# Attention without a shifted copy of V: another order of scores, turns of 64x64, and another order of work in the last pair

## The chip, the cores and the metric

The kernel runs on one core of one Trainium2 chip. Its time is device microseconds of one launch. The text uses these engine names: PE is TensorE (matmul; PEld is its weight load), DVE is VectorE, ACT is ScalarE, POOL is GpSimd, SP is SyncE, which here only issues DMAs.

## The reference, cut to what matters

One decoder layer in float32: 2048 positions, width 1024, 16 attention heads of 64 and 16 SSD heads of 64. Attention is causal, with windows of 128 steps at dilations 1, 4 and 16; the three results are mixed by their softmax sums.

```python
def dilated_window_attention(q, k, v, slopes, dilation):
    # positions are split into `dilation` residue sequences, blocks of 128;
    # a block of queries sees its own block of keys and the one before
    scores = jnp.einsum('bnqrhe,bnkrhe->bnrhqk', qb, kk).astype(jnp.float32)
    ...
    valid = (jk >= 0) & (steps >= 0) & (steps <= ATT_STEPS)
    scores = jnp.where(valid[:, None, None], scores + bias, -jnp.inf)
    lse = jax.nn.logsumexp(scores, axis=-1)
    p = jnp.exp(scores - lse[..., None]).astype(vv.dtype)
    o = jnp.einsum('bnrhqk,bnkrhe->bnqrhe', p, vv)

def reference(x, w_in, ...):
    proj = jnp.einsum('bsd,de->bse', x, w_in[layer])
    q, k, v, z_att, z_ssm, xbc, dt_raw = jnp.split(proj, list(SPLITS), axis=-1)
    ...   # three dilations, o1 to o3 and l1 to l3
    wts = jax.nn.softmax(jnp.stack([l1, l2, l3], axis=0), axis=0)
    y_att = wts[0][..., None] * o1 + wts[1][..., None] * o2 + wts[2][..., None] * o3
    y_att = rms_norm(y_att.reshape(Bsz, S, D_ATT) * jax.nn.silu(z_att), att_norm_g[layer])
    ...   # conv, silu, ssd_chunked
    y_ssm = rms_norm(y.reshape(Bsz, S, D_SSM) * jax.nn.silu(z_ssm), ssm_norm_g[layer])
    out = jnp.einsum('bse,ed->bsd', jnp.concatenate([y_att, y_ssm], axis=-1), w_out[layer])
    x = layer_norm(alpha * x + out, ln_g[layer], ln_b[layer])
```

## The kernel before

The program has three stages. The first, up to about 1148 us, makes all projections, the convolution and the SSD branch, and leaves q, k, v, the gates, the SSD rows (`d_us`) and the prepared output weights (`d_wo`) in DRAM. The change does not touch it.

The second is the attention. It goes over eight pairs of heads, and in each pair over the three dilations `d` = 0, 1, 2 (strides 16, 4, 1), four quarters `qd` and two halves `half`: 192 steps of two blocks of 128 queries for two heads. The order of all engines is the order of the code. The loop handles the scores of step i, the turns of step i-2 and the values of step i-3. A step works thus:

- `scores` (L947): q times k into two PSUM banks `S`, one per head. Head h lies in the rows 64h to 64h+63 of the array and the half a of a query block in the columns 64a to 64a+63, so these matmuls are 64x64 and there are four places in the array for them. A block in the first position of its sequence has 128 keys; any other has 192 here, since each half of 64 queries sees three blocks of 64 keys. The half a=0 sees the keys -2, -1, 0 and a=1 sees -1, 0, 1 (in blocks of 64).
- DVE adds the table of slopes and takes the row minimum (L953), ACT takes the exponential and its sum (L962).
- `transposes`: four turns of 128x128 through the identity into a bank `T` (L976), copied by DVE to `PT` (L978). The third block of 64 keys of both query blocks (columns 128 to 255 of `P`) needs two more turns per step, one per head (L984), copied to `PC` (L987). Only steps with a block that is not first have them.
- `values` (L1002): `PT` and `PC` times v into two banks `N`, then ACT or DVE copies them to `num`. For `PC` to meet the right rows of v, v is there twice: `v` as it is and `vs`, shifted by 64 positions.

The loads of `v` and `vs` are 1 MB each, issued by POOL or SP. Between steps the loop also places, for the pair before, the mixing weights: `statistics` and `gather` (sums to DRAM and back in another layout), `weights` (DVE, ACT, POOL), `broadcast` (the weights read back over 64 partitions each), `combine` (POOL; in the last pair DVE) and `keep_u` (the finished rows to `d_ua`). `broadcast` begins with a one-element memset on DVE (L1087), which takes the buffer `wb`; that buffer may still be on its way to `d_ua`.

The third stage is the output product. 64 products (`product`, L1201 to L1203, 24 matmuls of 512 columns each) take 16 blocks of 128 positions times an SSD half and an attention half of the width times two halves of the output. The first eight are the SSD halves of blocks 0 to 3; they need `split` (a rounded part by ACT, L1167, and the rest by DVE or POOL, L1169) and the weights 8 to 15. The ninth is the attention half of block 0; it needs all of the last pair's `combine`. `load_w` brings the weights into buffers of the attention as those come free, on POOL's queue.

## Time and profile before

| What | Value |
|---|---|
| time, median of 3 runs | 2009.96 us (2007.39 to 2012.77) |
| profiled execution, its own time | 2003.82 us |
| its span | 2002.0 us |
| PE busy in the span | 1945.7 us, 97% |
| DVE, ACT, POOL busy | 64%, 56%, 50% |
| DMA | 447.67 MB, mean 224 GB/s |

The profile is one execution. A busy PE means that a matmul is under way, and in fp32 two matmul records stand for one matmul instruction (one for a turn in transpose mode). The timeline merges neighbouring instructions of one line, so a row's start tells more than its length: the time from one row's start to the next is what the work took on PE.

### The profile page before, as it was taken

Reading aid. Unit: us, or ns where it says so; the run is one execution under the profiler, and the core shown is the slowest. Engines: PE = TensorE matmul, PEld = TensorE weight load, DVE = VectorE, ACT = ScalarE, POOL = GpSimd, SP = SyncE. Lnnn points to the kernel's source line nnn. Section 1 sums busy time; section 2 is a strip of 40 time slices with the busy share of each in tenths; the row PEclk is TensorE's granted clock in tenths of the full one; section 3 lists DMA queues with packets and bytes.
Section 4 is the critical chain, followed back from the end, with each engine's and each line's share of the span. In section 5 each row is a group of like instructions: output and inputs, shape, how many; then the busy total and the mean of one; then the engine's idle time right before and its main releaser. Section 6 shows DMA issues by size and latency. Waiting matters only on the chain.

```text
span 2002.0 us, 42714 instructions
## 1 busy us (share of the span) xinstructions
PE 1945.7 (97%) x16008; PEld 1588.2 (79%) x16008; DVE 1275.8 (64%) x3204; ACT 1120.0 (56%) x3036; POOL 998.3 (50%) x877
## 2 busy tenths in 40 slices
PE   8999999999999999999999999999999888999998
PEld 7888899888888888988888877777777666888886
DVE  7655376887766655644454388888887736655553
ACT  5454343566556774456566488988888732322220
POOL 0366514666556667155565343676776622432221
PEclk9999999999999999999999999999999998999999
DMA  6788676566787876888888766888888988332210
GB/s 270 236 284 293 213 280 227 159 195 190 237 306 266 279 245 239 312 269 256 272 277 259 256 228 165 229 244 235 252 238 254 265 242 260 134 102 92 92 61 32
DMA packets 260656, 447.67 MB, mean 224 GB/s; under 512 B 44785, under 2 KB 146673, under 8 KB 249057
## 3 DMA queue, kind: packets, MB, share of 16 engines
q1 hardware_dynamic: 170912, 205.39, 32.2%
q0 software_dynamic: 39088, 142.54, 21.6%
q10 hardware_dynamic: 50448, 97.01, 15.7%
q8 instruction: 126, 2.06, 0.4%
q14 instruction: 82, 0.66, 0.1%
HBM read 301.85 MB, written 151.39 MB: 226 GB/s over the span
## 4 chain that ended last, share of the span: by engine, by line
PE 85%; DVE 5%; DMA 4%; ACT 3%; issue 2%; POOL 1%; SPq 0%; ACTq 0%; DVEq 0%; POOLq 0%
PE pp L260 13%; PE pp L264 13%; PE pp L262 13%; PE N L1002 7%; PE S L947 6%; PE T L976 5%; PE pp L309 4%; PE S L1201 4%; PE S L1203 4%; PE S L1202 3%; PE ss L309 2%; PE T L1201 2%; PE T L1203 2%; PE T L1202 2%; PE ss L627 2%
## 5 line engine op out<-in xcount | busy, mean ns | idle before, releaser
L217 POOL TENSOR_TENSOR w<-wr,w 128x512 fp32r<-128x512 f32 x217 | 285.6, 1327 | 268.2 <-ACT w L216 184.0
L962 ACT ACTIVATE P<-P,st 128x192 f32<-128x192 f32 (+1 forms) x768 | 323.4, 423 | 59.9 <-DVE st L953 55.4
L252 ACT COPY ev<-pp 128x512 f32<-128x512 f32 x200 | 117.1, 587 | 315.3 <-PE pp L264 281.5
L953 DVE CUSTOM_DVE_ANT_0 P<-S,tb 128x192 f32<-128x192 f32 (+1 forms) x768 | 205.8, 324 | 53.6 <-PE S L947 44.1
L272 DVE TENSOR_TENSOR ev<-pp,ev 128x512 f32<-128x512 f32 x152 | 101.2, 686 | 140.6 <-PE pp L264 95.9
L216 ACT CAST w<-wr 128x512 fp32r<-128x512 f32 x224 | 134.1, 620 | 23.5 <-DVE wr L211 11.9
L962 ACT ACTIVATION_READ_ACCUMULATOR P<-P,st 128x1 f32 x768 | 145.0, 189 | 0.0
L1111 POOL TENSOR_TENSOR wb<-num,wb 128x2048 f32<-128x2048 f32 x21 | 95.7, 4558 | 93.7 <-DMA wb<-d_wd 90.2
L978 DVE COPY PT<-T 128x512 f32<-128x512 f32 x192 | 131.7, 686 | 3.8 <-PE T L976 3.8
L976 PE MATMUL T<-ident,P 128*128 128x128 f32 x768 | 127.3, 288 | 6.7 <-DVE PT L978 4.5
L1002 PE MATMUL N<-PT,v 128*64 128x64 f32 (+1 forms) x1536 | 124.5, 259 | 4.2 <-DVE PT L978 3.5
L976 PEld LDWEIGHTS T<-ident,P 128*128 128x128 f32 x768 | 81.3, 141 | 52.9 <-ACT P L962 16.8
L211 DVE TENSOR_TENSOR wr<-wr 128x512 f32<-128x512 f32 x128 | 112.2, 877 | 9.3 <-DMA wr<-w 5.9
L947 PE MATMUL S<-k,ex 64*64 64x192 f32 (+1 forms) x2048 | 108.8, 322 | 3.2 <-issue 3.2
L1002 PEld LDWEIGHTS N<-PT,v 128*64 128x64 f32 x1536 | 79.4, 138 | 38.3 <-issue 22.7
L459 DVE SCALAR_TENSOR_TENSOR ss<-U,cw,ss 128x512 f32<-128x512 f32 x144 | 106.0, 752 | 2.9 <-ACT ss L455 0.6
L1177 DVE TENSOR_REDUCE tb<-P 128x128 f32<-128x1024 f32 x30 | 60.2, 2006 | 45.1 <-ACT P L1174 21.1
L1239 POOL TENSOR_TENSOR k<-k,wb 128x1024 f32<-128x1024 f32 x8 | 25.8, 3225 | 122.0 <-DVE k L1238 122.0
L587 ACT ACTIVATE mt<-csb,wdr 128x128 f32<-128x128 f32 x256 | 78.9, 395 | 0.9 <-PE ss L627 0.8
L947 PEld LDWEIGHTS S<-k,ex 64*64 64x64 f32 x2048 | 66.4, 134 | 15.4 <-issue 8.9
L596 DVE TENSOR_TENSOR mt<-mt,ss 128x1024 f32<-128x1024 f32 x32 | 39.0, 1220 | 54.1 <-ACT mt L592 53.7
L260 PE MATMUL pp<-TT4h,w 128*128 128x512 f32 x176 | 69.6, 395 | 0.0
(493 smaller groups left out, 5991.1 us busy)
## 6 DMA issues: line engine op xcount, KB each, us to landing
wr<-w ACTq DMA_DIRECT2D x164, 256.0 KB
d_wc<-w SPq DMA_DIRECT2D x48, 512.0 KB
w<-d_wc POOLq DMA_DIRECT2D x48, 512.0 KB, 6.4
wb<-d_wd SPq DMA_DIRECT2D x48, 512.0 KB
d_wo<-wot POOLq DMA_DIRECT2D x32, 512.0 KB, 4.3
csb<-d_cs ACTq DMA_DIRECT2D x32, 512.0 KB
d_wv<-w SPq DMA_DIRECT2D x14, 1024.0 KB
w<-d_wv POOLq DMA_DIRECT2D x14, 1024.0 KB, 8.7
```

What stands on the lines that cost most here:

```text
L216: nc.scalar.copy(h, r)
L217: low.tensor_tensor(l, r, h.bitcast(F32), op=OP.subtract)
L260: nc.tensor.matmul(ps, w[:, 0, k], th[:, k], start=start and k == 0, stop=False, skip_group_check=not start)
L262: nc.tensor.matmul(ps, w[:, 0, k], tl[:, k], start=False, stop=False, skip_group_check=not start)
L264: nc.tensor.matmul(ps, w[:, 1, k], th[:, k], start=False, stop=(k == 3), skip_group_check=not start)
L309: nc.tensor.matmul(o, (th, tl)[j == 1][:, k, t], w[:, int(j == 2), k], start=start and r % 2 == k == j == 0, stop=(k == 3 and j == 2), ski ...
L947: nc.tensor.matmul(o, A["q"][d][64 * h:64 * h + 64, blk, 64 * a:64 * a + 64], kv, start=True, stop=True)
L953: nc.vector.tensor_tensor_reduce(P[:, h, cs], sp[h][:, cs], t, -0.125, 3.0e38, OP.add, OP.min, accum_out=stat(A, 0, d, h, blk))
L962: nc.scalar.activation(p, p, AF.Exp, bias=stat(A, 0, d, h, blk), scale=-1.0, accum_out=stat(A, 1, d, h, blk))
L976: nc.tensor.transpose(tp[:, h, i], P[:, h, 256 * i:256 * i + 128], ident)
L978: nc.vector.tensor_copy(pt, tp)
L1002: nc.tensor.matmul(o, l, r, start=start, stop=True, skip_group_check=True)
```

## The change

`vs` goes, with its loads and its shifted tables. Each half of a query block now lays its three blocks of keys in another order: a=0 as -2, -1, 0 as before, a=1 as 0, 1, -1. So the scores of a=1 are two matmuls, of 128 and of 64 columns, where there was one of 192; those of 64 columns come after the four wide ones of the block. The third block of keys now lies for half a in the rows 64a, and is turned with matmuls of 64x64 against the identity (two heads, two blocks, two halves: eight of them) instead of two turns of 128x128. `N` is now one bank per half a, and the copies to `num` follow that.

Around it: `keep_u` moves from the step (1,0,0) to (0,0,1). In the last pair the weights 8, 9 and 10 go to the three `vs` buffers during pairs 5 and 6, others move; the SSD rows of blocks 0 to 3 are fetched in the attention loop and block 0 is split there from the end of dilation 4; `zt7` is loaded there too; the weights' broadcasts go ahead of `keep_u` and of residuals 2 and 3; the residuals go through SP instead of ACT; and block 3 is split after the first `combine` step instead of after the third.

```diff
-        def load_v(A, x, d, queue=nc.gpsimd):
+        def load_v(A, d, queue=nc.gpsimd):
...
         def keys(A, d, qd, bq, h, a):
...
-            lo, hi = (j, j + 2 * w) if f else (j + w * (a - 2), j + w * (a + 1))
-            k = k[:, 4 * bq:4 * bq + 4, lo:hi] if d == 1 else k[:, :, lo:hi]
-            return k.rearrange("p r (c j) -> p c r j", j=4)
+            parts = [(0, j, j + 2 * w)] if f else [(0, j, j + 2 * w), (128, j - w, j)] if a else [(0, j - 2 * w, j + w)]
...
         def scores(A, d, qd, half):
...
-                for h in range(2):
-                    for a in range(2):
-                        o, kv = sp[h][64 * a:64 * a + 64, cs], keys(A, d, qd, 2 * i + half, h, a)
...
+                for n in range(2):
+                    for h in range(2):
+                        for a in range(2):
+                            for c0, c1, kv in keys(A, d, qd, 2 * i + half, h, a)[n:n + 1]:
...
         def transposes(d, qd, half, P):
...
-            tc_ = psT.tile([128, 2, 2, 128], F32, name="T")
+            tc_ = psT.tile([128, 2, 2, 64], F32, name="T")
             for h in range(2):
-                nc.tensor.transpose(tc_[:, 0, h], P[:, h, 128:256], ident)
-            pc = io.tile([128, 2, 128], F32, name="PC", bufs=2)
-            rows = slice(64 * new[0], 128)
-            nc.vector.tensor_copy(pc[rows], tc_[rows, 0])
+                for i in range(new.start, new.stop):
+                    for a in range(2):
+                        r = slice(64 * a, 64 * a + 64)
+                        nc.tensor.matmul(tc_[r, h, i], P[r, h, 192 * i + 128:192 * i + 192], ident[r, r],
+                                         start=True, stop=True)
+            pc = io.tile([128, 2, 2, 64], F32, name="PC", bufs=2)
+            nc.vector.tensor_copy(pc[:, :, new], tc_[:, :, new])
...
-                    if pr > 1 and at == (1, 0, 0):
+                    if pr > 1 and at == (0, 0, 1):
                         keep_u(pairs[pr - 2], nc.sync)
...
+                    if pr == 7:
+                        if at == (1, 1, 0):
+                            free.append(big("q_0"))
+                            X = big("ex", F32)
+                            for j in range(2):
+                                fetch_raw(j, 1, X[:, j * D:j * D + D])
+                        if at in ((1, 2, 1), (1, 3, 0)):
+                            split(0, 1, slice(4 - 4 * half, 8 - 4 * half), (0,))
+                        if at == (2, 0, 0):
+                            split(0, 1, parts=(1,))
...
+                        if at in ((2, 2, 1), (2, 3, 0)):
+                            fetch_raw(qd, 1)
...
                 if i == 2:
-                    for j in range(2):
-                        scaled(j)
-                    add(*adds.pop(0))
-                    add(*adds.pop(0))
-                    for j in range(3):
-                        combine(A, j)
+                    combine(A, 0)
                     load_w(0, 0, "num")
...
                         os_.insert(0, big("k_1", F32))
+                        broadcast(A, 0)
                         for n in range(2):
                             residual(n)
+                        broadcast(A, 1)
+                        broadcast(A, 2)
+                        keep_u(pairs[6], nc.sync)
+                        for n in range(2, 4):
+                            residual(n)
+                    if i == 3:
+                        for n in range(2):
+                            scaled(n)
+                        add(*adds.pop(0))
+                        add(*adds.pop(0))
+                        combine(A, 1)
+                        load_w(1, 0, "num")
+                        combine(A, 2)
```

How this stands on the engines is shown at three places.

On PE, one step of dilation 1 late in the last pair, before: from the scores of one step to the values of another (`S`, `T` and `N` are PSUM banks, `PT` and `PC` the turned scores).

```order
L947 MATMUL S<-k,ex 64x192 x8
L976 MATMUL T<-ident,P 128x128 x4
L984 MATMUL T<-ident,P 128x128 x2
L1002 MATMUL N_19558<-PT,v 64x64 x2
L1002 MATMUL N_19558<-PT,vs 64x64 x2
L1002 MATMUL N_19559<-PT,vs 64x64 x2
L1002 MATMUL N_19559<-PT,v 64x64 x2
L1002 MATMUL N_19558<-PC,v 64x64 x2
L1002 MATMUL N_19559<-PC,vs 64x64 x2
L1002 MATMUL N_19558<-PC,vs 64x64 x2
L1002 MATMUL N_19559<-PC,v 64x64 x2
```

And now. The five rows of scores shown are those of the step's second block; the same five stand ahead of them for its first block.

```order
L947 MATMUL S<-k,ex 64x192
L947 MATMUL S<-k,ex 64x128
L947 MATMUL S<-k,ex 64x192
L947 MATMUL S<-k,ex 64x128
L947 MATMUL S<-k,ex 64x64 x2
L976 MATMUL T<-ident,P 128x128 x4
L987 MATMUL T<-ident,P 64x64 x8
L1009 MATMUL N_20774<-PT,v 64x64 x2
L1009 MATMUL N_20775<-PT,v 64x64 x2
L1009 MATMUL N_20774<-PT,v 64x64 x2
L1009 MATMUL N_20775<-PT,v 64x64 x2
L1009 MATMUL N_20774<-PC,v 64x64 x2
```

The scores grew from 8 matmuls to 12, the extra turns from two of 128x128 to eight of 64x64; the values are 16 matmuls as before.

On DVE, after the attention: the rows from the last of the mixing weights (`cm`) over the `combine` products (`wb<-num,wb`) to the split of block 3 (`num<-P,num`), before.

```order
L1080 TENSOR_TENSOR cm<-cm,mm 128x3x32
L1177 TENSOR_REDUCE tb_19839<-P 128x128
L1212 RECIPROCAL st<-st 128x1 x2
L1218 SCALAR_TENSOR_TENSOR k<-S,st,k 128x512 x2
L1111 TENSOR_TENSOR wb<-num,wb 128x2048 x2
L1115 TENSOR_TENSOR wb<-wb 128x2048
L1169 TENSOR_TENSOR num<-P,num 128x1024
```

And now, where the split of block 3 is `q<-P,q`.

```order
L1085 TENSOR_TENSOR cm<-cm,mm 128x3x32
L1181 TENSOR_REDUCE tb_20975<-P 128x128
L1216 RECIPROCAL st<-st 128x1 x2
L1115 TENSOR_TENSOR wb<-num,wb 128x2048
L1173 TENSOR_TENSOR q<-P,q 128x1024
L1222 SCALAR_TENSOR_TENSOR k<-S,st,k 128x512 x2
L1115 TENSOR_TENSOR wb<-num,wb 128x2048
L1119 TENSOR_TENSOR wb<-wb 128x2048
```

The split stands behind one `combine` product instead of two and a sum.

On SP, the DMAs at the end of the attention, before: the SSD rows (`d_us`), the statistics, the weights out and their broadcasts in.

```order
L1155 DMA P<-d_us_108 128x512
L1155 DMA P<-d_us_109 128x512
L1055 DMA d_st_119<-sT 16x16x8 x4
L1081 DMA d_wd_127<-cm 128x3x32
L1089 DMA wb<-d_wd_127 64x2048 x6
```

And now, with `d_ua` the rows of pair 6 and `xc` the residuals, which both were on ACT's queue.

```order
L1060 DMA d_st_119<-sT 16x16x8 x4
L1086 DMA d_wd_127<-cm 128x3x32
L1095 DMA wb<-d_wd_127 64x2048 x2
L1185 DMA k<-xc 128x1024 x2
L1095 DMA wb<-d_wd_127 64x2048 x2
L1095 DMA v<-d_wd_127 64x2048 x2
L1102 DMA d_ua<-wb 128x16x128
L1185 DMA ex<-xc 128x1024 x2
```

The first broadcast stands right behind the weights, and the store of `d_ua` and two residuals behind all broadcasts.

More of the change, by code (lines that the diff above doesn't have):

```diff
@@ L920, in cols @@
         def cols(d, qd, half, i):
-            w = 128 if first(d, qd, 2 * i + half) else 192
-            return slice(384 - w, 384) if i else slice(0, w)
+            return slice(192 * i, 192 * i + (128 if first(d, qd, 2 * i + half) else 192))
         def keys(A, d, qd, bq, h, a):
@@ L1004, in values @@
                 m = at(2 * i + half)
+                if d == 0:
+                    for h in range(2):
+                        mm(out(i, h), v[:, m, 64 * h:64 * h + 64], pt[:, h, i], half == 0)
+                    continue
+                f = first(d, qd, 2 * i + half)
+                for a in range(2):
+                    for h in range(2):
+                        mm(out(i, h, a), v[:, m if f else m - 1 + a, 64 * h:64 * h + 64],
+                           pt[:, h, i, 64 * a:64 * a + 64], half == i == 0)
+            for i in range(2):
                 if first(d, qd, 2 * i + half):
-                    for h in range(2):
-                        mm(out(i, h, 0, 128), v[:, m, 64 * h:64 * h + 64], pt[:, h, i], half == 0)
                     continue
@@ L1010, in values @@
                     for h in range(2):
[L1011 to L1021 removed]
+                        r = slice(64 * a, 64 * a + 64)
+                        mm(out(i, h, a), v[r, at(2 * i + half) - a, 64 * h:64 * h + 64], pc[r, h, i], False)
             if half == 1:
@@ L1296, in hybrid_layer @@
                         if pr == 7:
-                            for e in range(12, 16):
+                            for e in (14, 15):
                                 load_w(e, 1)
@@ L1316, in hybrid_layer @@
                         load_z(pairs[pr - 1])
-                    if pr == 7 and at in ((2, 0, 1), (2, 1, 0)):
-                        split(0, 1, slice(4 * qd, 4 * qd + 4), (0,))
-                    if pr == 7 and at == (2, 1, 0):
-                        split(0, 1, parts=(1,))
+                    if pr == 7:
[8 more added lines that the diff above has]
+                            split(0, 1, parts=(1,))
+                            zt7 = cm_.tile([128, NR, NJ], F32, name="num", bufs=6)
+                            nc.sync.dma_start(f2(zt7), d_za[7])
+                        if at in ((2, 2, 1), (2, 3, 0)):
+                            fetch_raw(qd, 1)
+                    if not half:
+                        for e, hf, name in LOADS.get((pr, d, qd, 0), ()):
+                            load_w(e, hf, name)
+                    if pr == 7 and at == (2, 0, 0):
+                        free.append(big("num"))
                     if at in STEPS:
@@ L1331, in hybrid_layer @@
                         permute(pairs[pr + 1], 1)
[L1332 to L1343 removed]
+        with tc.manual_schedule(engines={E.PE, E.DVE, E.Activation, E.Pool, E.SP}):
             A = pairs[7]
```

116 lines of the change are left out of this document (44 added, 72 removed).

## The prediction

> **What bounds the kernel now.** I read the windows first, cut where the stages of the trace change: attention, the passage to the output products, the products. The columns are the stretch, its length, busy time and instruction count of PE, PEld, DVE, ACT and POOL, PE's granted clock, the DMA share and GB/s.
>
> ```profile
> 1148.00:1596.00 448.00, 431.72 (x8082) 320.06 (x8082) 372.52 (x1898) 385.19 (x1717) 284.95 (x239) 1.00 0.81 233
> 1596.00:1673.00 77.00, 59.08 (x346) 46.21 (x344) 36.55 (x47) 20.46 (x34) 27.35 (x26) 0.84 0.93 261
> 1673.00:2002.00 329.00, 319.28 (x1403) 258.76 (x1401) 179.45 (x243) 78.73 (x112) 89.68 (x37) 0.99 0.30 99
> ```
>
> In the attention PE is busy 431.7 of 448 us, ACT 385 and DVE 373. So PE bounds it, with 16.3 us idle at most to be won, and work added on PE lengthens it while DVE and ACT have room. The passage is different: PE is idle 18 us of 77 and its clock is at 0.84. In the products PE is full again and the change adds nothing there.
>
> Next, PE's timeline for one full step of a smaller dilation, from its scores to the next step's scores (columns: start, length, engine, line, operation, count; rows left out are more of the same values).
>
> ```profile
> 1361.69 0.83 PE L947 MATMUL S<-k,ex 64*64 64x192 f32 x16
> 1362.46 0.66 PE L976 MATMUL T<-ident,P 128*128 128x128 f32 x4
> 1362.95 0.38 PE L984 MATMUL T<-ident,P 128*128 128x128 f32 x2
> 1363.27 0.34 PE L1002 MATMUL N<-PT,v 128*64 128x64 f32 x4
> ...
> 1363.88 0.27 PE L1002 MATMUL N<-PC,v 64*64 64x64 f32 x2
> ...
> 1364.16 0.85 PE L947 MATMUL S<-k,ex 64*64 64x192 f32 x16
> ```
>
> No row has a wait, so the differences of starts are prices: scores 0.77, four turns 0.49, two turns 0.32, PT values 0.61, PC values 0.28, in all 2.47 us. A step of the first dilation has no extra turns, and there the four turns are followed at once by the values:
>
> ```profile
> 1334.47 0.65 PE L976 MATMUL T<-ident,P 128*128 128x128 f32 x4
> 1335.06 0.66 PE L1002 MATMUL N<-PT,v 128*64 128x128 f32 x8
> ```
>
> That is 0.59 for the same four turns, 0.10 more. The difference is that the next matmul has another shape of stationary block (128*64 after 128*128). So **a change of shape costs 0.10**. It lies in 0.32 and 0.61 too, but not in 0.28, since PC values and scores are both 64*64. Then eight matmuls of 64 columns cost 0.51 where two run at once (PT, two column halves) and 0.28 where four do (PC, four quarters): 0.23 for four groups more, 0.058 a group.
>
> **The turns.** Two turns of 128x128 become eight of 64x64, row half a to column half a, so two places of the array are used and two can run at once. The nearest row is PT: eight matmuls of 64 columns, two at a time, and a change of shape behind them, 0.61. That takes the place of 0.32: +0.29. Ahead of them is a new change of shape, 128*128 to 64*64: +0.10. The trace doesn't show such turns; from below they cost 0.28+0.10 = 0.38 in place of 0.32 (four at a time, as PC), from above they go one at a time, eight groups of 0.058 more than PT, 1.07 in place of 0.32. I take 0.61, because row halves 0 and 1 are the only two places used.
>
> **The scores.** The a=1 place takes 128 and then 64 columns beside 192 of a=0. Whether the places keep separate queues is seen in a step with only one extra block:
>
> ```profile
> 1358.96 0.27 PE L1002 MATMUL N<-PC,vs 64*64 64x64 f32 x2
> 1358.99 0.38 PE L947 MATMUL S<-k,ex 64*64 64x192 f32 x2
> 1359.07 0.22 PE L1002 MATMUL N<-PC,vs 64*64 64x64 f32 x2
> 1359.13 0.28 PE L1002 MATMUL N<-PC,v 64*64 64x64 f32 x4
> ```
>
> Here scores of the next step (row half 0) begin while six PC records (row half 1), ahead of them in the program, are still to come. So row halves run apart. For column halves no row shows it. If they run apart too, the extra matmuls lie beside the wide ones: 0 to 0.05 a step. If not, four groups of 0.058 a step are added: 0.23. I take 0.03, near the row.
>
> A full step then costs 0.29+0.10+0.03 = 0.42 more. How many steps:
>
> ```profile
> L984 PE MATMUL T<-ident,P x224: 270/273/474, 1175.8 to 1609.6; 128*128 128x128 f32 x112
> ```
>
> 224 turns, two a step, are 112 steps; eight of them (one per pair, the first of dilation 1) have only one such block and I count 0.2 for each. So 104 x 0.42 + 8 x 0.2 = 45.3, and 16 steps of first blocks, whose values now come in halves, bring it to **+46 us**. Bounds: 0.16 a step (turns 0.38, scores free) to 1.08 (turns 1.07, scores 0.23), +18 to +117; with turns at 0.61 not over 0.62 a step, +66. DVE and ACT keep their instructions: same columns, same copies; their 373 and 385 us hide in a longer PE time.
>
> **The loads of vs and keep_u.** The loads of `vs` are 16 of 1 MB or less; they leave POOL's and SP's queues. What reaches PE of the DMA traffic is shown by the waits of DVE and PE from 1160 to 1590 us (total, times, longest) and by one place on PE:
>
> ```profile
> DVE wb L1087 <- DMA d_ua<-wb: 9.4, 4, 2.6
> DVE mm L1069 <- DMA cm<-d_st: 3.4, 4, 1.3
> PE N L1002 <- DVE PT L978: 3.5, 3, 1.7
> 1351.98 0.63 PE L976 MATMUL T<-ident,P 128*128 128x128 f32 x4 [1.32 <-DVE PT L978]
> 1408.56 0.63 PE L976 MATMUL T<-ident,P 128*128 128x128 f32 x4 [1.74 <-DVE PT L978]
> ```
>
> The memset L1087 waits for the store of the finished rows, and behind it on DVE stand the minima and the PT copy for which PE's turns wait 1.3 to 1.7 us. `keep_u` now goes out seven steps earlier, ahead of the table load and the broadcasts on SP, so this wait should go: -5 of 9.4, since PE feels less than DVE. What is late next there is PE itself. The wait for `cm` depends on two trips through DRAM and on the steps of the first dilation, which stay as long as they are; with less traffic -2 of 3.5. Together **-7** (0 to -13).
>
> **The passage.** PE's rows from the last scores to the first attention product (the ninth), with the eighth product's start for a length:
>
> ```profile
> 1594.71 1.05 PE L947 MATMUL S<-k,ex 64*64 64x192 f32 x16
> 1600.26 0.50 PE L1203 MATMUL S<-k,num 128*128 128x512 f32 x1 [3.23 <-POOL num L1169]
> 1659.55 0.80 PE L1203 MATMUL S<-k,num 128*128 128x512 f32 x1 [12.04 <-DVE num L1169]
> 1667.66 0.48 PE L1201 MATMUL S<-k,num 128*128 128x512 f32 x1
> 1673.35 0.39 PE L1201 MATMUL S<-num 128*128 128x512 f32 x1
> ```
>
> From last scores to ninth product 78.6 us. The work in it is eight products of 5.69 (1667.66 to 1673.35), 45.5, and the rest of the attention, about 6 with the new prices (scores 0.77, two times turns 1.2, three times values 0.89): 51.5. So 27 us is all that can be won. Both large waits are for a split's rest: of block 0 on POOL, which is now done a dilation earlier, and of block 3 on DVE. But the ninth product has a chain of its own:
>
> ```profile
> 1614.04 2.80 SPq L1055 DMA_DIRECT2D d_st<-sT  x4
> 1624.60 0.38 SPq L1081 DMA_DIRECT2D d_wd<-cm  x1
> 1633.60 3.17 SPq L1089 DMA_DIRECT2D wb<-d_wd  x4
> 1646.81 2.29 DVE L1111 TENSOR_TENSOR wb<-num,wb 128x2048 f32<-128x2048 f32 x1 [9.23 <-DMA wb<-d_wd]
> 1653.74 2.29 DVE L1111 TENSOR_TENSOR wb<-num,wb 128x2048 f32<-128x2048 f32 x1 [4.64 <-DMA wb<-d_wd]
> 1658.28 1.22 DVE L1169 TENSOR_TENSOR num<-P,num 128x1024 fp32r<-128x1024 f32 x1
> 1672.04 1.23 DVE L1169 TENSOR_TENSOR num<-P,num 128x1024 fp32r<-128x1024 f32 x1 [1.16 <-ACT num L1167]
> ```
>
> Statistics out at 1614.0, weights out at 1624.6, their broadcasts only at 1633.6 (9.0), the first used at 1646.8 (13.2), block 0 ready at 1673.3, just when PE arrives. So taking away the 12 us wait alone would win little: **the chain is late next**. Mid-kernel the same two DMAs take less:
>
> ```profile
> 1335.81 0.36 SPq L1081 DMA_DIRECT2D d_wd<-cm  x1
> 1339.02 1.13 SPq L1089 DMA_DIRECT2D wb<-d_wd  x2
> 1565.68 1.12 SPq L1089 DMA_DIRECT2D wb<-d_wd  x2
> 1573.15 4.53 POOL L1111 TENSOR_TENSOR wb<-num,wb 128x2048 f32<-128x2048 f32 x1 [11.16 <-DMA wb<-d_wd]
> ```
>
> 3.2 and 7.5. With broadcasts ahead of residuals and of `keep_u`, and more weights loaded before, I take these: 10.6 (statistics to weights) + 3.2 + 7.5 + 26.5 of DVE less its 4.64 of waiting = 43. The statistics now stand behind one whole product on PE, so they start 6 + 5.7 after the last scores, and the ninth product comes at 55: 23 won. With 9.0 and 13.2 unchanged it is 67: 12 won. **-23** (-12 to -27).
>
> **Sum.** 46 - 7 - 23 = **+16 us** on an execution of 2003.8 us (span 2002.0). That one lies 6 us below the median of the runs, 2010.0, and below their lowest; the difference is carried over to the median: **2026 us**.
>
> **Rivals.** *One pass for a turn.* A turn in transpose mode is one record (224 for 224), a plain matmul two. If the 64x64 turns took one, four groups of 0.058 fall away in each step: 108 x 0.23 = -25, so 46-25-7-23 = -9, about 2001. Against it: the code calls a plain matmul, as for the values. It decides once the eight turns cost under 0.46 a step (16 us over 108 steps less than 0.61). The Trainium skill, "TensorEngine Tiling (Array Packing)", section "Tile-to-Partition Mapping", says that column tiling excludes transpose mode with fp32 input; by that this rival falls, and no row here shows it.
>
> *Turns one at a time.* Before, the two row halves always write different PSUM banks (scores by head, PC by block). The new turns of both halves go into one bank `T`. If such matmuls exclude each other, the eight turns are 16 groups and not 8: 108 x 0.46 = +50, about 2076. For it: no row shows two row halves in one bank. Against: they write different partitions. The same page, section "Restrictions and Gotchas", says that different row tiles cannot use one bank at the same time; by that rule this would be the case, and no row here shows it either way.
>
> *Scores in step.* Column halves share a queue: +0.20 x 108 = +22, 2048; a passage that wins 12 gives 2037.
>
> *Nothing in sum.* If the lighter traffic takes all 16 us of PE's idle time in the attention and the passage wins 27: 46-16-27 = +3, 2013. For it: DMA at 0.81 of its time. Against: most of PE's waits there are for DVE and ACT or for no DMA. That the change would not shorten the passage at all (a late weight, say) gives +39.
>
> **Chances.** Forecast 0.52 (2018 to 2036), scores or passage worse 0.12 (to 2050), one at a time 0.09: all slower. Nothing in sum 0.14, one pass 0.10, and one pass with all waits gone 0.03, which are faster. So faster 0.13, same 0.14, slower 0.73, where 0.3% (6 us) is about what a measurement can tell. The range leaves out one at a time and the fast end: 2002 to 2050.
>
> **What would show it.** A full step of 2.89 us on PE; T to 64x64 turns 0.59, these to the values 0.61, scores 0.77 to 0.82; no wait at the memset; no wait of PE for L1169's successor beyond 3 us; the ninth product some 55 us after the last scores. Turns of 0.38 or 1.07, or scores near 1.0, would make it wrong.

## The result, and the profile after

The changed kernel takes 2068.5 us (median of 4 runs, 2064.5 to 2069.0) against 2008.8 us before (median of 4 runs): a ratio of 1.029, 95% interval 1.027 to 1.031. It is slower by about 60 us, where +16 was forecast. The profiled execution took 2068.88 us, span 2067.1.

Starts of PE's rows cut the two profiled executions into the same stages (us):

| Stage | before | after | difference | forecast |
|---|---|---|---|---|
| begin to first scores | 1148.4 | 1145.7 | -2.7 | 0 |
| first to last scores (attention) | 446.3 | 527.5 | +81.2 | +39 |
| last scores to ninth product (passage) | 78.6 | 63.8 | -14.8 | -23 |
| ninth product to last matmul | 319.4 | 320.9 | +1.4 | 0 |

So the attention holds the miss, 42 us too long, and the passage 8 us. The windows of the changed kernel, cut at its stages (stretch, length, busy time and instructions of PE, PEld, DVE, ACT, POOL, granted clock, DMA share, GB/s):

```profile
1148.00:1673.00 525.00, 487.43 (x10508) 395.24 (x10507) 367.99 (x1885) 387.92 (x1716) 285.85 (x236) 0.95 0.63 181
1673.00:1737.00 64.00, 54.90 (x430) 44.01 (x429) 34.49 (x48) 19.54 (x35) 10.06 (x14) 0.95 0.72 199
1737.00:2067.00 330.00, 320.74 (x1400) 259.66 (x1400) 180.40 (x243) 78.85 (x113) 90.46 (x38) 0.99 0.30 101
```

DVE, ACT and POOL do the work they did. PE has some 2400 more matmul records in the attention, and it is idle 38 us of 525 (16 of 448 before) at a clock of 0.95 (1.00 before). So part of the excess is not work. A step that nothing disturbs is on PE's timeline:

```profile
1379.79 0.85 PE L947 MATMUL S<-k,ex 64*64 64x192 f32 x24
1380.57 0.66 PE L976 MATMUL T<-ident,P 128*128 128x128 f32 x4
1381.16 0.68 PE L987 MATMUL T<-ident,P 64*64 64x64 f32 x16
1381.77 0.69 PE L1009 MATMUL N<-PT,v 128*64 128x64 f32 x16
1382.38 0.46 PE L1009 MATMUL N<-PC,v 64*64 64x64 f32 x16
1382.67 0.65 PE L947 MATMUL S<-k,ex 64*64 64x192 f32 x13
```

Scores 0.78, four turns 0.59, eight small turns 0.61, values 0.61 and 0.29: 2.88 us, and 2.89 was forecast. What the forecast hasn't is this, on the same timeline:

```profile
1502.51 0.33 PE L1009 MATMUL N<-PC,v 64*64 64x64 f32 x4
1505.65 0.39 PE L1009 MATMUL N<-PC,v 64*64 64x64 f32 x10 [2.81 <-issue]
1505.93 1.25 PE L947 MATMUL S<-k,ex 64*64 64x128 f32 x18
```

PE stands in the middle of one line, between the fourth and the fifth of sixteen records, and "issue" says that it waited for no semaphore. Behind it 18 score records take 1.25 us where 24 took 0.85: the granted clock is 0.5 from 1506.0 to 1509.4. PE's waits of this kind from 1160 us to 1650 after and to 1590 before (total, times, longest), after first:

```profile
PE N L1009 <- issue: 16.9, 8, 3.6
PE S L947 <- issue: 4.1, 3, 3.0
PE T L987 <- issue: 3.9, 3, 2.6
```
```profile
PE S L947 <- issue: 3.5, 4, 1.4
PE N L1002 <- issue: 1.2, 2, 0.7
PE T L976 <- issue: 0.4, 1, 0.4
```

24.9 us after, 5.1 before, and the clock stands at 0.5 for 51 us of the attention after (10.2 of these belong to a wait for `sT`, below), 3.4 before. Two more long stops of the changed kernel carry another name:

```profile
1309.17 1.12 PE L976 MATMUL T<-ident,P 128*128 128x128 f32 x4 [3.07 <-ACT P L962]
1371.17 0.68 PE L987 MATMUL T<-ident,P 64*64 64x64 f32 x16 [2.24 <-DVE PT L978]
```

The work named had ended 0.6 and 0.8 us before PE went on, so it is not what PE waited for last. Without these two, PE's waits put down to DVE and ACT are 1.2 us in this stretch; before they were 10.9. What PE waits for is in the page's list of DMA queues (packets, MB, share), after and then before:

```profile
q8 instruction: 146, 2.39, 0.5%
```
```profile
q8 instruction: 126, 2.06, 0.4%
```

2.39 MB in 146 packets are 16 KB each, and PE and PEld with their semaphore records have 37460 records after: 257 a packet. They have 5055 fewer before, and the queue 20 packets fewer: 253 a packet. So a packet is about 256 instructions of PE. A full step had 108 instructions in 2.47 us and now has 152 in 2.88: a packet lasts 5.84 us before, 4.85 us after. The packet records of the trace show the rest. Counted in packets used, no packet starts before a fixed point, and PE runs dry 1.16 packets beyond that point. It does so at all nine stops of 2.2 to 3.6 us, the two with another name among them: at each a packet starts between 0.7 us before and 0.7 us after PE stands still (at 1503.04 here), and PE goes on 2.5 to 3.0 us after that start. The delay from that point to a packet's start has a median of 3.5 us before and 2.9 after, nine in ten are under 6.0 and 6.1, and the longest are 7.1 and 10.3. So delivery is hardly slower but for the longest delay; PE uses instructions up faster.

A second new stop lies in the last pair (PE, ACT and POOL of the timeline):

```profile
1654.02 0.66 PE L976 MATMUL T<-ident,P 128*128 128x128 f32 x4
1660.58 1.12 PE L987 MATMUL T<-ident,P 64*64 64x64 f32 x16 [5.90 <-ACT sT L1051]
1658.50 1.06 ACT L1178 ACTIVATE ex<-ex 128x1024 f32<-128x1024 f32 x1 [5.16 <-POOL q L1173]
1656.13 2.33 POOL L1173 TENSOR_TENSOR q<-ex,q 128x1024 fp32r<-128x1024 f32 x1
```

The small turns need a bank that the copies of the statistics (L1050, L1051) have to empty; on ACT these stand behind the squares of SSD block 0 (L1178), which wait until POOL has made that block's low half. With the clock at 0.5 until 1666.4 this stop costs 5.9 + (1666.4 - 1660.6)/2 = 8.8 us.

The chain to the ninth product, from SP's, DVE's, ACT's and PE's rows:

```profile
1697.92 0.38 SPq L1086 DMA_DIRECT2D d_wd<-cm  x1
1699.64 1.13 SPq L1095 DMA_DIRECT2D wb<-d_wd  x2
1706.88 15.07 SPq L1185 DMA_DIRECT2D ex<-xc  x2
1706.98 2.29 DVE L1115 TENSOR_TENSOR wb<-num,wb 128x2048 f32<-128x2048 f32 x1 [6.26 <-DMA wb<-d_wd]
1714.58 2.29 DVE L1115 TENSOR_TENSOR wb<-num,wb 128x2048 f32<-128x2048 f32 x1 [2.85 <-DMA wb<-d_wd]
1729.74 0.75 DVE L1222 SCALAR_TENSOR_TENSOR ex<-S,st,ex 128x512 f32<-128x512 f32 x1 [6.42 <-ACT ex L1188]
1728.65 1.06 ACT L1188 ACTIVATE ex<-ex 128x1024 f32<-128x1024 f32 x1 [17.12 <-DMA ex<-xc]
1737.06 0.79 PE L1205 MATMUL S<-num 128*128 128x512 f32 x1 [8.66 <-ACT num L1171]
```

Broadcasts go out 1.7 us behind the weights and the first is used 7.3 us later, about as forecast (3.2 and 7.5). But DVE then waits 6.4 us for residual rows that come late, and PE waits 8.7 us.

### The profile page after: what moved, and what is told of

It is laid out like the page before. It is cut to its first block, busy times and chain, and to the rows that moved or that the text cites. A ratio compares the mean times of both kernels' runs of the same rounds, so it can differ in the third digit from the quotient of the medians.

```text
span 2067.1 us, 47757 instructions
## 1 busy us (share of the span) xinstructions
PE 1999.9 (97%) x18536; PEld 1662.3 (80%) x18536; DVE 1269.4 (61%) x3204; ACT 1121.8 (54%) x3036; POOL 985.8 (48%) x866
## 3 DMA queue, kind: packets, MB, share of 16 engines
q8 instruction: 146, 2.39, 0.5%
## 4 chain that ended last, share of the span: by engine, by line
PE 90%; DMA 4%; DVE 3%; issue 2%; ACT 2%; POOL 1%; SPq 0%; ACTq 0%; POOLq 0%; DVEq 0%
PE pp L260 14%; PE pp L264 13%; PE pp L262 13%; PE N L1009 8%; PE S L947 6%; PE T L976 5%; PE pp L309 4%; PE S L1205 4%; PE S L1207 3%; PE S L1206 3%; PE T L987 3%; PE ss L309 2%; PE T L1205 2%; PE T L1206 2%; PE T L1207 2%
## 5 line engine op out<-in xcount | busy, mean ns | idle before, releaser
L1009 PE MATMUL N<-PT,v 128*64 128x64 f32 (+1 forms) x2560 | 134.1, 244 | 10.1 <-issue 10.1
L1115 POOL TENSOR_TENSOR wb<-num,wb 128x2048 f32<-128x2048 f32 x21 | 95.3, 4539 | 78.6 <-DMA wb<-d_wd 77.4
L1009 PEld LDWEIGHTS N<-PT,v 128*64 128x64 f32 x2560 | 100.4, 141 | 34.8 <-issue 18.2
L947 PE MATMUL S<-k,ex 64*64 64x128 f32 (+2 forms) x2912 | 113.7, 283 | 4.2 <-issue 4.1
L947 PEld LDWEIGHTS S<-k,ex 64*64 64x64 f32 x2912 | 96.9, 138 | 13.2 <-issue 8.7
L987 PE MATMUL T<-ident,P 64*64 64x64 f32 x1728 | 79.2, 232 | 12.0 <-ACT sT L1051 5.9
L987 PEld LDWEIGHTS T<-ident,P 64*64 64x64 f32 x1728 | 63.0, 141 | 31.1 <-issue 17.1
L1243 POOL TENSOR_TENSOR k<-k,v 128x1024 f32<-128x1024 f32 x8 | 25.8, 3223 | 119.2 <-DVE k L1242 119.2
```

Source lines behind the costliest of these rows:

```text
L947: nc.tensor.matmul(o, A["q"][d][64 * h:64 * h + 64, blk, 64 * a:64 * a + 64], kv, start=True, stop=True)
L987: nc.tensor.matmul(tc_[r, h, i], P[r, h, 192 * i + 128:192 * i + 192], ident[r, r], start=True, stop=True)
L1009: nc.tensor.matmul(o, l, r, start=start, stop=True, skip_group_check=True)
```

## The experiments

**Theory A**: PE's instruction packets stand behind the broadcasts of the weights; more instructions in each microsecond of PE turn the same delays into stops of 3 us and half clocks. That they stand behind them is the theory; which DMA engine a packet waits at is not on record. Its rivals: the order of loads makes the stops; they are waits for data. Eighteen kernels were run, each beside the kernel before on the same chip.

| Run | time, us | ratio to before, 95% | attention | passage |
|---|---|---|---|---|
| attn_only | 2064.3 | 1.028 to 1.031 | 515.6 | 71.3 |
| sched_only | 2009.2 | 1.000 to 1.003 | 461.6 | 73.9 |
| before_split | 2043.3 | 1.017 to 1.021 | 487.6 | 75.9 |
| after_scores1 | 2048.7 | 1.020 to 1.023 | 507.6 | 62.8 |
| after_few_bc | 2025.5 | 1.009 to 1.012 | 482.7 | 63.5 |
| before_few_bc | 1977.5 | 0.984 to 0.987 | 425.7 | 71.0 |
| after_pieces | 2047.5 | 1.017 to 1.023 | 509.2 | 63.9 |
| before_pieces | 2030.7 | 1.010 to 1.015 | 465.1 | 89.7 |
| after_halves | 2063.8 | 1.026 to 1.030 | 521.8 | 63.7 |
| before_halves | 2007.5 | 1.000 to 1.002 | 453.4 | 77.9 |
| after_2kb | 2060.1 | 1.024 to 1.030 | 515.3 | 63.7 |
| before_2kb | 2010.7 | 1.001 to 1.003 | 455.4 | 77.3 |
| keep_only | 2011.2 | 1.002 to 1.005 | 453.5 | 78.7 |
| after_latekeep | 2071.2 | 1.030 to 1.034 | 529.5 | 63.8 |
| after_dve_split | 2064.4 | 1.028 to 1.033 | 523.7 | 63.7 |
| after_resid | 2066.6 | 1.029 to 1.032 | 521.1 | 62.1 |
| sched_latekeep_pieces | 2023.3 | 1.008 to 1.011 | 471.5 | 79.3 |
| sched_latekeep_resid | 2009.9 | 1.001 to 1.003 | 455.7 | 71.5 |

### The two halves of the change

`attn_only` is the kernel before with the functions `load_v`, `keys`, `scores`, `transposes`, `values` and the table of the change. `sched_only` is the kernel before, attention included, with the change's order behind the last scores and its earlier store, but without the early cast of SSD block 0. In it is this of the change:

```diff
-                    if pr > 1 and at == (1, 0, 0):
+                    if pr > 1 and at == (0, 0, 1):
                         keep_u(pairs[pr - 2], nc.sync)
...
+                    if at in ((2, 2, 1), (2, 3, 0)):
+                        fetch_raw(qd, 1)
...
+                        broadcast(A, 0)
                         for n in range(2):
                             residual(n)
+                        broadcast(A, 1)
+                        broadcast(A, 2)
```

> The kernel before with nothing of the change but the new attention (score order, 64x64 turns, values without shifted V, its loads and table). Theory A: the new step gives PE 152 instructions in 2.88 us where it had 108 in 2.47, so a packet of 256 instructions is used up in 4.85 us and not 5.84, and the next one, that needs up to 6 us or more when broadcasts are under way, comes too late: PE stands for 2.5 to 3.8 us some ten times and then runs at a clock of 0.5 for some us. Then the last scores come about 80 us later than before (46 of them step price), the passage stays at about 78 us, and the time is 2080 to 2092 us. Rival S: the standstills come from the changed order of loads in the last pairs and from the earlier store of finished rows, not from the attention itself: then only the step price is left, last scores 44 to 50 us later, no gap of PE beyond 1.7 us, 2050 to 2058 us.

> The kernel before, with its own attention (shifted V, two 128x128 turns), and of the change the earlier store of finished rows, the broadcasts of the last pair ahead of residuals and store, the fourth block fetched and split sooner and the rest of the order behind the last scores; the early cast of the first SSD block is left as before. Theory A: the attention has no new standstill, last scores 0 to 5 us earlier than before; from last scores to ninth product 55 to 65 us in place of 78.6: 1985 to 1998 us. Rival S (the new order disturbs the attention): last scores 10 us later or more, 2005 us or more. Rival N (the passage was shortened in the changed kernel only because the attention ended later): passage over 74 us, 2003 to 2010 us.

The attention alone carries the whole loss (2064.3 against 2068.5), with 23.1 us of PE's waits for "issue". So the stops come with it and not with the order of loads, as theory A says, though the time is 16 us under its range: passage and stops both came out smaller. The order alone wins nothing: its passage is 4.8 us shorter, its attention 15 us longer. That was a miss; the sections on the earlier store and on the chain take it up.

### The number of instructions, with the DMAs left alone

`before_split` cuts the score matmuls of the kernel before; `after_scores1` puts those of the changed kernel together; their keys then lie in another order than table and turns expect, so it is a kernel for its time alone.

```diff
-                        nc.tensor.matmul(o, A["q"][d][...], kv, start=True, stop=True)
+                        n = kv.shape[1]
+                        for c in ((0, n),) if cs.stop - cs.start == 128 else ((0, 2 * n // 3), (2 * n // 3, n)):
+                            nc.tensor.matmul(o[:, c[0]:c[1]], A["q"][d][...], kv[:, c[0]:c[1]], start=True, stop=True)
```
```diff
-            parts = [(0, j, j + 2 * w)] if f else [(0, j, j + 2 * w), (128, j - w, j)] if a else [(0, j - 2 * w, j + w)]
+            parts = [(0, j, j + 2 * w)] if f else [(0, j - w, j + 2 * w)] if a else [(0, j - 2 * w, j + w)]
```

> The kernel before with one thing more: each score matmul of 192 columns is cut into one of 128 and one of 64. A full step then has 140 PE instructions in place of 108; columns, DMAs and all other engines' work stay. Theory A: the steady step takes 2.5 to 2.7 us, a packet of 256 instructions is used up in 4.6 to 4.9 us, and gaps of 2.5 to 3.8 us with a half clock behind them appear where broadcasts run, as in the changed kernel: beyond the step price (104 steps by what is measured, 3 to 24 us) 25 to 45 us more, 2035 to 2070 us. Rival S or any theory in which the number of instructions doesn't matter: only the step price, 2010 to 2033 us, no gap beyond 1.7 us.

> The changed kernel with the score matmuls of the second row half in one piece of 192 columns again (eight matmuls fewer in a full step, 136 instructions in place of 152); the keys then stand in another order than table and values take them, which the result shows and no time. Theory A: the step takes 2.83 to 2.88 us, so a packet is used up in 5.3 to 5.4 us in place of 4.85, halfway back to the 5.84 of before: gaps and half clock shrink to about half, last scores 10 to 22 us sooner of which at most 5 are step price: 2047 to 2060 us. Rival S (instruction number doesn't matter): only the step price, 2063 to 2069 us.

PE's rows of `before_split`, two starts of full steps and a stop (the last with PE's half clock behind it):

```profile
1323.27 0.95 PE L949 MATMUL S<-k,ex 64*64 64x128 f32 x32
1325.85 0.95 PE L949 MATMUL S<-k,ex 64*64 64x128 f32 x32
...
1441.00 0.56 PE L949 MATMUL S<-k,ex 64*64 64x128 f32 x8 [3.50 <-issue]
1441.48 1.01 PE L978 MATMUL T<-ident,P 128*128 128x128 f32 x4
```

The step takes 2.58, 0.11 more, so its price is 104 x 0.11 = 12 us. The kernel is 37 us slower, and its PE waits for "issue":

```profile
PE N L1004 <- issue: 16.6, 9, 3.9
PE S L949 <- issue: 15.8, 9, 3.6
PE T L986 <- issue: 1.0, 1, 1.0
```

33.4 us in place of 5.1, with no DMA, no column and no other engine's work changed. In `after_scores1` the step is only 0.02 shorter (2 us in all), yet 20 us are won: the clock stands at 0.5 for 27 us in place of 51, PE's stops over 1 us in the attention add up to 27 in place of 32. Both results lie in theory A's ranges and outside the rival's. The number of instructions by itself brings the stops, with the transfers left as they are.

### The broadcasts

`after_few_bc` and `before_few_bc` leave out nearly all bytes of the broadcasts of pairs 0 to 6; all positions are then multiplied by the weights of sixteen, so these too are kernels for their time alone:

```diff
+            if A["pr"] < 7:
+                w1 = A["w1", d] = cm_.tile([128, 16], F32, name="w1", bufs=3)
+                for h in range(2):
+                    nc.sync.dma_start(w1[64 * h:64 * h + 64], dap(d_wd[A["pr"]], (d * 2 + h) * S, [[0, 64], [1, 16]]))
+                return
```

> The changed kernel, in which pairs 0 to 6 broadcast only the weights of 16 positions (64 bytes a packet) and multiply all 2048 positions by these; so nearly all of the bytes of the broadcasts are left out, PE's instructions and POOL's multiplications stay. Theory A: an instruction packet is late because it stands behind the broadcasts' packets on the same 16 DMA engines; without them its longest delay falls from 10.3 us to under 6, the gaps of PE over 2 us go but for the one at sT (1654 us), half clock in the attention falls from 51 us to under 20: last scores 20 to 30 us sooner, 2038 to 2050 us. Rival Q: delivery is late whatever else runs: 2060 us or more, gaps as before. Rival P (POOL's queue or the waits for the broadcasts): gaps go only where POOL is waited for, of which the trace shows none: same as Q.

> The kernel before with the same cut as the changed kernel had: pairs 0 to 6 broadcast the weights of 16 positions only and multiply all positions by these. Theory A: at 5.84 us a packet the old attention loses little to late packets, so it wins much less than the 45 us that the changed kernel won: last scores 8 to 20 us sooner than before (gaps and waits for broadcasts), 1986 to 1998 us. The difference of the two kernels without broadcasts is then the step price, 40 to 50 us between the first and the last scores. Rival Q (broadcasts cost both kernels the same, for instance by POOL's waits): 40 us or more sooner here too, 1960 to 1970 us, and the difference of the two stays at 70 us or more.

The windows of the attention, `after_few_bc` and then `before_few_bc`:

```profile
1148.00:1628.00 480.00, 469.01 (x10501) 380.61 (x10502) 365.87 (x1886) 386.69 (x1714) 286.06 (x236) 0.99 0.48 153
```
```profile
1148.00:1571.00 423.00, 421.55 (x8026) 315.35 (x8025) 367.26 (x1883) 381.31 (x1710) 284.79 (x239) 1.00 0.62 197
```

In the old attention PE is now idle 1.5 us of 423 and has no wait for "issue" left in the list; in the new one 2.9 us are left of 24.9, and the longest delay of a packet fell from 10.3 to 5.7 us. So the broadcasts cost 44.8 us of the attention after (527.5 - 482.7) and 20.7 before (446.3 - 425.7): more in both than expected, and 24 us more after. Without them the two attentions differ by 57.1 us; 9.9 of these are the stop at `sT` (7.4 us and its half clock), and 47.2 are left for the steps, where 46 was forecast. So the 81.2 us are 47.2 (steps), 9.9 (`sT`) and 24.1 (broadcasts). They add up by the way they are taken; what tests them is that 47.2 meets the price read from rows. The 20.7 us before are late packets only in part: there the broadcasts also bring the waits for data.

### Broadcasts cut or spread

Three ways to keep the bytes: eight DMAs a broadcast of one block of 512 columns each (`pieces`, packets of 2 KB in place of 8 KB), the second half one step later on ACT's queue (`halves`), and four DMAs with 2 KB packets (`2kb`).

```diff
-                nc.sync.dma_start(f2(wb[64 * h:64 * h + 64]), dap(d_wd[A["pr"]], (d * 2 + h) * S, [[0, 64], [1, S]]))
+                for c in range(0, S, 512):
+                    nc.sync.dma_start(f2(wb[64 * h:64 * h + 64])[:, c:c + 512],
+                                      dap(d_wd[A["pr"]], (d * 2 + h) * S + c, [[0, 64], [1, 512]]))
```
```diff
-                        broadcast(pairs[pr - 1], d + (at == (1, 2, 0)))
+                        broadcast(pairs[pr - 1], d + (at == (1, 2, 0)), (0,))
+                    if pr and at in ((0, 3, 1), (1, 1, 0), (1, 2, 1)):
+                        broadcast(pairs[pr - 1], d + (at == (1, 2, 1)), (1,), nc.scalar)
```
```diff
+                for c in range(2):
+                    nc.sync.dma_start(f2(wb[64 * h:64 * h + 64]).rearrange("p (n c k) -> p n c k", c=2, k=512)[:, :, c],
+                                      dap(d_wd[A["pr"]], (d * 2 + h) * S + 512 * c, [[0, 64], [1024, 2], [1, 512]]))
```

> The changed kernel with each broadcast of weights cut into four column pieces, so that its packets are of 2 KB and not of 8 KB; PE's instructions are the same. Theory A with the long packets as the cause of late delivery: an instruction packet stands behind several 8 KB packets of 0.63 us each; with 2 KB packets its longest delay falls from 10.3 us to under 5, the gaps of PE of 2.5 to 3.8 us go, most of the half clock with them: 2030 to 2048 us. Rival Q: instruction packets are late because of the bytes ahead of them, not because of their cut: gaps stay, 2062 to 2074 us. Rival P (the gaps have nothing to do with the DMAs): no gap goes, same time; the eight issues on SP in place of two may then even cost some us.

> The kernel before with each broadcast of weights in four column pieces (packets of 2 KB in place of 8 KB), nothing else. Theory A with long packets: before, too, has gaps of 1 to 1.7 us where an instruction packet is late (its longest delay is 7.1 us); these gaps go, last scores 2 to 8 us sooner: 1997 to 2004 us. Rival: at 5.84 us a packet the delivery is just in time, nothing to win, 2004 to 2009 us; or SP's eight issues in place of two make broadcasts later and POOL's combines with them: 2009 us or more.

> The changed kernel with the same halves of broadcasts. Theory A (the number of packets that stand ahead decides): the longest delay falls from 10.3 us to under 6.5, gaps over 2.5 us go, half clock in the attention falls from 51 us to 20 to 30: 2035 to 2052 us. Rival (the bytes per time decide, however they are spread): 2062 us or more.

> The kernel before; of each broadcast of pairs 0 to 6 the second half (64 of 128 rows) goes out one step later, on ACT's queue, so that at most four packets of 8 KB and not eight stand at a DMA engine at once. Theory A: the longest delay of an instruction packet falls from 7.1 us to under 5.5, the gaps of 1 to 1.7 us go: 1994 to 2003 us. Rival: little was lost to gaps before, and ACT pays for its 24 issues or waits for the broadcasts: 2004 to 2015 us.

> The changed kernel with the same cut. With eight issues it won 21 us. Theory V: with half the issues 20 to 32 us sooner, 2037 to 2049 us, gaps over 2.5 us only at sT. Rival: the packets that stand ahead are as many bytes as before and the delay stays, 2055 us or more.

> The kernel before; each broadcast of pairs 0 to 6 in four DMAs of two column blocks each, so that its packets are of 2 KB at half of the eight issues that the cut into single blocks took on SP (there 5 to 9 us a broadcast, and the old attention became 19 us longer). Theory V: what made that run slow was SP's issues, which let POOL's combines and its reordered queries come late; with half of them and short packets the longest delay of an instruction packet is under 6 us, last scores 5 to 15 us sooner than before, 1991 to 2002 us, faster than both kernels. Rival: four issues are late enough, 2005 to 2020 us; or the short packets save nothing, 2002 to 2008 us.

`after_pieces` won the 21 us that were expected, though its longest delay of a packet fell to 8.0 us and not under 5, and in `before_pieces` PE's waits for "issue" fall from 5.1 to 0.9 us. But that kernel lost 26 us: its passage is 11 us longer, and its PE waits for the queries that POOL reorders, which come late now:

```profile
PEld S L947 <- POOL ex L912: 9.5, 14, 1.7
PE S L947 <- POOL ex L912: 6.6, 8, 1.5
```

That the pieces make them late, through SP's eight issues, was expected as a rival and is not shown by a run of its own. The other two were to keep the gain without that price, and both missed: the changed kernel's times are 5 and 8 us lower with them, which their intervals do not set apart from it, and in the kernel before they won nothing (1.0009 and 1.0021). The longest delay of a packet stayed at about 9 and 10 us after. Short packets alone are therefore not what helped `after_pieces`; there SP takes 5 to 6 us to issue a broadcast, and what spreads the bytes over time may be that. No run separates the two.

### The earlier store

`keep_only` has only the move of `keep_u` to (0,0,1); `after_latekeep` is the changed kernel with it moved back.

> The kernel before with nothing of the change but the store of finished rows seven steps earlier. Theory K: without the wait of the memset the three broadcasts of a pair run closer upon the loads, the longest delay of an instruction packet rises as in the run with the new order (9.3 us, 7.1 before), and PE gets gaps of 2 to 3.3 us with half clocks: last scores 8 to 15 us later than before, 2012 to 2022 us. Rival W (the forecast's term): the wait of DVE and the late PT copies go, nothing comes in their place: last scores 3 to 7 us sooner, 1999 to 2004 us. Rival L: the later last scores of that run came from the loads of its last pair: the first seven pairs as before, 2004 to 2009 us.

> The changed kernel with the store of finished rows at its old place (first step of the second dilation). In the kernel before the earlier store cost 6.5 us. Theory K (it packs the broadcasts of a pair closer): it costs in the changed kernel too, 4 to 10 us of the attention: 2058 to 2065 us. Rival W (the forecast's term): the memset's wait comes back and with it 3 to 7 us: 2071 to 2076 us. Rival: the longer steps leave room for both: 2066 to 2070 us.

In the kernel before, the move that was forecast to win 5 us costs 6.5 (interval 1.002 to 1.005). The memset's wait does go, but PE waits for "issue" instead:

```profile
PE S L947 <- issue: 5.4, 3, 2.2
PE N L1002 <- issue: 3.9, 4, 1.7
PE T L976 <- issue: 2.3, 1, 2.3
```

11.6 us, 5.1 before; the time lies 1 us under theory K's range. In the changed kernel the two places can't be told apart (2071.2 and 2068.5; their intervals to the kernel before overlap), so theory K's gain there did not come.

### The stop at sT

```diff
-                (nc.gpsimd if (n, br) == (0, 1) else nc.vector).tensor_tensor(
+                nc.vector.tensor_tensor(
```

> The changed kernel with the low half of the first SSD block made on DVE in place of POOL (line 1174), so that the squares of that block, which stand ahead of the statistics' copies on ACT, don't wait for POOL. Theory B: PE's wait of 5.9 us for sT at 1654 us and the 10.2 us at half clock behind it go, 8 to 12 us: 2055 to 2061 us. Rival: PE then waits at the same place for something else (POOL's or a late packet), under 4 us won: 2064 to 2069 us.

Theory B failed as tried: the copies of the statistics are on time now, but the stop only changed its place. DVE, PE and POOL of that kernel's timeline:

```profile
1652.01 7.02 DVE L1173 TENSOR_TENSOR q<-ex,q 128x1024 fp32r<-128x1024 f32 x1
1660.89 1.09 PE L976 MATMUL T<-ident,P 128*128 128x128 f32 x4 [5.48 <-DVE PT L978]
1653.42 4.52 POOL L1119 TENSOR_TENSOR wb<-wb 128x2048 f32<-128x2048 f32 x1
```

The subtraction that takes DVE 1.22 us elsewhere took 7.02: it ended 1.1 us after POOL's addition of 4.52 us, though it had begun 1.4 us ahead of it. That SSD block 0, split early, stands in PE's way is shown by both forms; `attn_only`, without it, has no stop for `sT` or for DVE there.

### The chain behind the last scores

```diff
                         broadcast(A, 1)
+                        for n in range(2, 4):
+                            residual(n)
                         broadcast(A, 2)
                         keep_u(pairs[6], nc.sync)
-                        for n in range(2, 4):
-                            residual(n)
```

`sched_latekeep_resid` and `sched_latekeep_pieces` are `sched_only` with `keep_u` at its old place, the first with this edit, the second with broadcasts in pieces; they were to be faster than both kernels.

> The changed kernel with the residual rows of blocks 2 and 3 asked for ahead of the third broadcast and of the store of the seventh pair's rows on SP. Theory R: of the chain to the ninth product 6.4 us are DVE's wait for the scaled rows of block 2 (an addition stands ahead of the sum of the third product there); with the rows there in time the ninth product comes 57 to 60 us after the last scores in place of 63.8: 2060 to 2064 us. Rival: the third broadcast comes later by as much as the rows come sooner, or the rows were late by their own transfer: 62 to 65 us, 2066 to 2070 us.

> The kernel before with its own attention, the store of finished rows where it was, whole broadcasts, and the change's order behind the last scores with the residual rows of blocks 2 and 3 asked for ahead of the third broadcast. If the earlier store and the cut broadcasts were what lengthened the attention in the two runs with this order (15 and 25 us), it is again 445 to 449 us; passage 66 to 71 us in place of 78.6: 1993 to 2001 us, faster than both kernels. Rival: the loads that the new order brings forward into the last steps lengthen the attention by 5 us or more: 2001 to 2008 us, no gain.

> The kernel before with its own attention, the store of finished rows where it was, broadcasts in four pieces, and the change's order behind the last scores (broadcasts first, fourth block split sooner). Theory A and K: no gap over 2 us in the attention (last scores 0 to 8 us sooner than before), passage 66 to 74 us in place of 78.6: 1989 to 2002 us, faster than both kernels. Rival: the ninth product waits for its rows as long as the fourth block's wait was, nothing is won in the passage: 2002 to 2009 us.

In `after_resid` the wait for residual rows is gone and DVE waits for the third broadcast instead:

```profile
1717.08 2.29 DVE L1115 TENSOR_TENSOR v<-num,v 128x2048 f32<-128x2048 f32 x1 [4.24 <-DMA v<-d_wd]
```

The passage is 1.7 us shorter, the time from the ninth product to the end 7 us longer. `sched_latekeep_resid` gives the same picture: 7 us won in the passage, 7 lost behind it (326.4), 9 lost in the attention, no gain. These 9 and the 7 that `keep_only` lost in its attention are about the 15 of `sched_only`; where the 9 come from stays open. `sched_latekeep_pieces` paid for the pieces as `before_pieces` did. No run that does the whole work beats the kernel before.

## Why the prediction was wrong, by its own steps

- **The turns and the scores: right.** Forecast 2.89 us a step, measured 2.88, each part within 0.02; in sum +46 forecast, +47 by the two kernels without broadcasts. *One pass for a turn* (under 0.46) and *turns one at a time* (1.07) fall with the 0.61 that was taken, *scores in step* (near 1.0) with 0.78. The rule of the Trainium skill, "TensorEngine Tiling (Array Packing)", section "Restrictions and Gotchas", that different row tiles cannot use one bank at once would, read as taking turns, have made these turns of both row halves into one bank take 1.07; the measured 0.61 speaks against that here.
- **"The loads of vs and keep_u", -7: the step that failed.** It says that what reaches PE of the DMA traffic is shown by the waits of DVE and PE for data, and prices only these. These waits went: neither the memset's nor that for `cm` is left, and PE's for DVE and ACT fell from 10.9 us to 1.2 (without the two stops that carry another name). But PE's own instructions come by DMA too. The kernel before already lost to that (5.1 us of "issue" in its list of waits, 20.7 us by `before_few_bc`, counting all that the broadcasts cost), and 152 instructions in 2.88 us in place of 108 in 2.47 raise that cost by 24 us, the won waits already taken off. So the term is +24 and not -7. A step's price was counted in PE time and not in instructions. The earlier store, priced at -5, is a loss of 6.5 in the kernel before.
- **The Trainium skill** had the mechanism: "Runtime: NRT & Kernel Launch", section "Instruction fetch mechanics", says that an engine's instructions are fetched in 16 KB blocks of 256 by a DMA queue of its own, as the 257 records a packet show. It adds that crossing a block's border is "mostly hidden"; here that holds without the bytes of the broadcasts (2.9 us of stops in the attention), and with them a border costs up to 3.6 us and mostly a half clock besides.
- **A term was missing**: the early cast of SSD block 0 was counted as a wait removed. It brings the stop at `sT`, 8.8 us here and 9.9 in `after_few_bc`.
- **The passage, -23: mis-sized**, measured -14.8. The statistics' turn on PE starts 14.0 us after the last scores (11.7 forecast), and the chain behind them takes 49.8 us and not 43. The two DMAs took 9.0 together (10.7 forecast); the 6.4 us of DVE waiting for residual rows behind `keep_u` on SP are not in it. The edit that lets them come in time shows that the third broadcast is late next.

In sum: 47 + 10 + 24 - 15, and the stages' -2.7 and +1.4, are the 65 us between the two profiled executions' last matmuls; the medians are 60 apart. The forecast was 46 - 7 - 23.

## What to carry to other kernels

Price a change of the matmul shapes twice, in engine time and in instructions per microsecond: here PE's many small instructions ran out when their packets came late beside the data, and a wait called "issue" in the middle of a line was the mark. A wait that the profile shows can also be what spaces the transfers; taking it away (the memset's here) may only move the stop. To price suspected traffic, run both kernels without it and compare the difference with the sum of the other terms.

## What was not expected of the hardware

- PE's cushion of instructions is thin: it ran dry 1.16 packets (some 300 instructions) after the point before which no packet starts. A delay of 6.1 us stopped it for 3.1 us where a packet lasts 4.85; before, where it lasts 5.84 and one delay in ten is over 6.0, no stop for "issue" was longer than 1.4 us.
- At eight of the nine stops of 2.2 to 3.6 us the granted clock was 0.5 for 3.4 or 6.8 us, from within the stop or up to 1.7 us behind it: 18 score records took 1.25 us where 24 take 0.85. At the stop at `sT` it was 0.5 for 10.2 us, from 1.5 us into the stop.
- A DVE subtraction with both inputs in SBUF took 7.02 us in place of 1.22 while POOL added in SBUF. The Trainium skill, "SBUF — State Buffer", section "Who interferes with whom", says that such a DVE instruction contends with a GpSimd instruction that reads SBUF, and calls the shared ports an exclusive lock; the row agrees in its end, 1.1 us after POOL's, and not in its start, 1.4 us ahead of POOL's, so its cause is not settled.
